# A feed-forward part with Strassen products: weight and token loads move from SyncE's DMA queue to GpSimd's, and forms and down pieces change their place in the order

## The chip, the cores and the metric

The kernel runs on one core of a Trainium2 chip. The metric is device time in microseconds of one execution, the median of three runs. One more execution was taken by the hardware profiler, and all rows below come from it.

## The reference

One inference step of a one-layer decoder trunk, all in float32: 2048 prompt tokens and 8 sample tokens (one for each of 8 sequences with 16384 cached positions in pages of 128).

```python
def layer(x, pos, conv_prev, chunk_len, attend, p):
    proj = rmsnorm(x, p['g_mix']) @ p['w_in']
    u, v, c_q, c_kv, k_rope = ...            # gelu, rmsnorm and rope of slices of proj
    out_a = rmsnorm(spatial_gate(u, v, ...), p['g_out_a'])
    out_b = rmsnorm(attend(q_nope, q_rope, c_kv, k_rope), p['g_out_b'])
    x = x + jnp.concatenate([out_a, out_b], axis=-1) @ p['w_out']
    f, conv_new = conv_ffn(x, conv_prev, p['g_ffn'], p['w_up'], p['w_conv'], p['b_conv'], p['w_down'])
    return x + f, c_kv, k_rope, v, conv_new

def conv_ffn(x, conv_prev, g_ffn, w_up, w_conv, b_conv, w_down):
    up = rmsnorm(x, g_ffn) @ w_up                      # 1024 -> 2*2816
    xp = jnp.concatenate([conv_prev, up], axis=1)
    c = b_conv
    for k in range(3):                                 # causal depthwise convolution
        c = c + xp[:, k:k + T] * w_conv[k]
    gate, val = c[..., :2816], c[..., 2816:]
    return (jax.nn.silu(gate) * val) @ w_down, xp[:, -2:]
```

For the sample tokens `attend` reads all 8 x 128 cached pages, through a page table.

## The kernel before

Tokens lie on the free axis, features on the partitions. Each float32 operand of a large product is split in a high part (`hi`, a rounded copy by ScalarE, L86) and a low part (`lo = x - hi`, by VectorE or GpSimd, L126), and each product is three matmuls: hi x hi, hi x lo, lo x hi. The stages follow one another: input projection, attention, output projection, feed-forward.

**The sample stream.** The attention of the sample tokens is spread through all stages by `fill`, which takes a step of it whenever matmuls of a planned length have been written. Its pages come through SyncE's DMA queue: each `pump` issues 16 page loads (`ct`, later `cn`) as soon as slots are free, and the first of them waits in the queue until TensorE has read the pages that lay there. The stream ends with the third of the four token blocks below.

**The feed-forward part** takes the tokens in four blocks (`BL`; 512 each, the last 520) and the 2816 gate and value columns in 22 steps of 128 (`NF`). A *unit* is one step of one block, 88 in all. The two weight slices of a unit (gate `graw`, value in two halves `vraw`) and the two halves of a block form a 2 x 2 system that is computed with seven products instead of eight (Strassen): each product has a *form* of the weights (`wu`) and one of the tokens (`B11`, `T2`, ...). The token forms are made once a block by `load_h2`, while the last unit of the block before runs. The weight forms are made in each unit anew by `split_w`: VectorE makes two sums (L1380 and L1381), GpSimd two differences (L1406, L1407), and for each of seven forms ScalarE makes the high part and GpSimd the low one.

**The order is written out by hand**, and each engine takes its instructions in that order. In `up`, behind product j of unit q, `rest(j)` writes in this order: deferred work of the gate chain that falls due at this product (`flush`), loads that are due (`later`, `dlater`), then weight forms until `AHEAD` products ahead of j are covered, then as many *pieces* as `PIECES` says, then steps of side work. The sums belong to the first form of the next unit and stand where that form is made.

The gate chain of a unit spreads over its products and over the next unit's (slot 7 is product 0 of the next unit): bias and taps of the convolution, `silu`, then the gate product and `gh` (L2014, L86) and `gl` (L2023). For the second half of a block these last three are in slots 10, 10 and 11.

```python
            at_slot(10, lambda: gmul(1), lambda: ghi(1))
            at_slot(11, lambda: glo(1))
```

Each pair of units (even and odd) is followed by eight pieces of the down projection (`dp`): a piece is six matmuls into 128 of the 1024 output rows, out of two PSUM buffers, and VectorE adds it to `y` (L1775). Pieces need `gh` and `gl` of both units. Their weights come by `load_d` in four loads a pair (`draw`, two buffers) and are split by `split_d` (`wdh`, `wdl`). `split_d` follows every second piece, one product later, and `load_d` follows it, again one product later. The last pair of a block has its pieces in `ending` (or `last_pieces`).

Queues: `sp` is SyncE's, `gq` GpSimd's, `aq` ScalarE's. A DMA is issued in its place in its engine's order, and waits there until its target is free. In the feed-forward part SyncE's queue has all raw weights, the token loads of `load_h2`, the pages, the block's inputs `y`, and the stores and reloads of finished blocks. In the last block `late` reloads the finished blocks, normalises them and stores them, through the same queue.

Of the raw weights, the second value half of unit q+1 has the shortest way: its load is written one product after the fifth form of unit q, and the sums that read it two products after the load.

Of the kernel before, what the change touches and what calls it, by code (L numbers as in the profile page):

```python
# [26 lines left out]
NF = FF // 128  # L27
# [9 lines left out]
T0, T1, T2, T3 = -8, -3, 3, 0  # L37
# [14 lines left out]
def build(tc, A):  # L52
# [15 lines left out]
    sp, aq, gq = Queue(nc.sync), Queue(nc.scalar), Queue(nc.gpsimd)  # L68
# [55 lines left out]
    def split_to(hi, lo, src, lo_eng=None):  # L124
        copy(hi, src)
        (lo_eng or dve).tensor_sub(lo, src, f(hi))  # L126
# [11 lines left out]
    def kslot(shape, name, dt=F32):  # L138
        return kv.tile(shape, dt, tag="k", bufs=6, name=name)

    def qslot(shape, name, dt=F32):
        return kv.tile(shape, dt, tag="q", bufs=2, name=name)
# [20 lines left out]
    with ExitStack() as B:  # L163
# [11 lines left out]
        xs = wp.tile([128, 8, NS], F32, name="xs")  # L175
# [307 lines left out]
        for k in range(8):  # L483
# [18 lines left out]
            t = h0  # L502
# [403 lines left out]
    with ExitStack() as Ax:  # L906
# [123 lines left out]
        for i in range(16):  # L1030
# [17 lines left out]
            for j in (0, 1) if i == 0 else (i,) if i > 1 else ():  # L1048
                p = pm.tile([128, 512], F32, tag="mm", name="pu")
                proj_a(p, *(HA[1] if j == 1 else (hh, hl)), 0)  # L1050
                act.activation(us[:, j % 2, :], p, AF.Gelu, scale=RC[j][:, 0:1])
            p = pm.tile([128, 512], F32, tag="mm", name="pv")
# [87 lines left out]
    with ExitStack() as At:  # L1140
# [19 lines left out]
        def load_v(h, r):  # L1160
            vt[h, r] = v = sb.tile([128, 4, 128], F32R, tag="v", bufs=6, name="v")
            gq.dma_start(out=v, in_=v_sp[r * 512:r * 512 + 512, h, :].rearrange("(j p) e -> p j e", p=128))
            yield
# [130 lines left out]
        for i in range(NT + DONE + int(DN)):  # L1294
# [30 lines left out]
            if i == 14:  # L1325
                p = psT.tile([128, 512], F32, tag="t", name="spt")
# [15 lines left out]
                next(ahead, 0)  # L1342

    FORMS = ("B11", "T2", "B21", "T3", "T1", "T4", "B22")
    PIECES = ((0, 0, 0, 0, 1, 1, 1), (1, 1, 1, 1, 1, 0, 0))
    BL = [(0, 256), (512, 256), (1024, 256), (1536, 260)]
    NB, AHEAD = len(BL), 5
    NU = NB * NF
    GATE, VAL, TMP, wts, later, dlater = {}, {}, {}, {}, [], []
    at = {"g": 0, "v": 0, "w": 0, "dl": 0, "ds": 0}  # L1350

    def load_g():
        q = at["g"]
        at["g"] += 1
        if q < NU:
            GATE[q] = qslot([128, 8, 128], "graw")
            (sp if q else gq).dma_start(out=GATE[q], in_=A["w_up"][q % NF, 0])

    def load_v():
        if not at["v"]:  # L1360
            at["v"] = 2
            t = qslot([128, 8, 128], "vraw")
            gq.dma_start(out=t, in_=A["w_up"][0, 1])
            VAL[0], VAL[1] = t[:, 0:4], t[:, 4:8]
            return
        q, a = divmod(at["v"], 2)
        at["v"] += 1
        if q < NU:
            VAL[2 * q + a] = t = sb.tile([128, 4, 128], F32, tag="vr", bufs=3, name="vraw")
            sp.dma_start(out=t, in_=A["w_up"][q % NF, 1, :, 4 * a:4 * a + 4, :])  # L1370

    def form(src):
        w = kslot([128, 2, 4, 128], "wu", F32R)
# [44 lines left out]
    def load_d():  # L1418
        i = at["dl"]
        at["dl"] += 1  # L1420
        if i < 4 * NU // 2:
            p, m = divmod(i, 4)
            fi = 2 * p % NF
            DR[i] = t = sb.tile([128, 2, 2, 128], F32, tag="dr", bufs=2, name="draw")
            sp.dma_start(out=t.rearrange("p j m n -> p j (m n)"),
                         in_=A["w_down"][fi * 128:(fi + 2) * 128, m * 256:m * 256 + 256].rearrange("(j p) n -> p j n", p=128))

    def split_d():
        i = at["ds"]
        at["ds"] += 1  # L1430
        if i < 4 * NU // 2:
            if i % (2 * NF) == 2 * NF - 2 or i == 4 * NU // 2 - 1:
                w = kslot([128, 2, 2, 2, 128], "wd", F32R)
                hi, lo = w[:, 0], w[:, 1]
            else:
                hi, lo = (sb.tile([128, 2, 2, 128], F32R, tag=t, name=t) for t in ("wdh", "wdl"))
            split_to(hi, lo, DR.pop(i), pool)
            wts["d", i] = hi, lo
            dlater.append(load_d)
# [10 lines left out]
    with ExitStack() as Po:  # L1450
# [88 lines left out]
        for j, ci in enumerate(seq):  # L1539
            for m in range(8):  # L1540
                if j > 0 or m > 3:
                    p = pm.tile([128, 512], F32, tag="mm", name="op")
# [30 lines left out]
    with ExitStack() as Fx:  # L1573
# [9 lines left out]
        def parts(b):  # L1583
            return ends(b) if b == NB - 1 else ((0, 512),)
# [3 lines left out]
        def load_h2(b):  # L1588
# [6 lines left out]
            def src(k0, nk, h):  # L1595
                return x2_sp[k0 * 128:(k0 + nk) * 128, c0 + h * hm:c0 + h * hm + hm].rearrange("(k p) t -> p k t", p=128)

            def new(n, dt):
                tag = slots.pop(0)
                return sb.tile([128, 4, 260], dt, tag=tag, bufs=1, name=n), tag  # L1600

            def raw(n, k=slice(0, 4)):
                if n not in raws:
                    raws[n] = new("r" + n, F32)
                return raws[n][0][:, k, 0:hm]
# [27 lines left out]
            def free(n):  # L1633
                slots.extend(old[n])
# [12 lines left out]
            if b == 0:  # L1647
# [3 lines left out]
                xs = temps()  # L1651
# [20 lines left out]
                    lo(n, eng)  # L1672
                return
            free("B11")
            sp.dma_start(out=raw("B11"), in_=src(0, 4, 0))
            R = load_r()
            yield
            free("T2")
            yield
            free("B21")  # L1680
            sp.dma_start(out=raw("B21"), in_=src(4, 4, 0))
            yield
            free("T3")
            sp.dma_start(out=raw("T3"), in_=src(0, 4, 1))
            yield
            free("T1")
            for k in range(4):
# [2 lines left out]
            free("T4")  # L1690
            xs = temps()
            for i in range(2):
                sp.dma_start(out=xs[i], in_=src(4 + 2 * i, 2, 1))
            for k in range(4):
                scale(raw("B21", k), raw("B21", k), 4 + k, 0)
            yield
# [69 lines left out]
        def pieces(b, fi, gts):  # L1766
            for m in range(8):
                w = wd(b, fi, m)
                if m == 0:
                    gts = [G[i] for i in gts]  # L1770
                for o, nn in parts(b):
                    p = pd.tile([128, 512], F32, tag="d", name="dp")
                    mm3(p[:, 0:nn], [(*w(j), gt[0][:, o:o + nn], gt[1][:, o:o + nn]) for j, gt in enumerate(gts)])
                    y = Y[b][m][:, o:o + nn]
                    dve.tensor_add(y, y, p[:, 0:nn])  # L1775
                    fill(6 * nn / 2.4)
                if m % 2:
                    dlater.append(split_d)
                yield
# [183 lines left out]
        def up(b, fi, it, side, slow, hs):  # L1963
# [22 lines left out]
            def rest(j):  # L1986
# [5 lines left out]
                while at["w"] <= 7 * q + j + AHEAD and at["w"] < 7 * NU:  # L1992
                    split_w()
                take(it, PIECES[odd][j])
                take(side, 1)
# [94 lines left out]
        for b in range(NB):  # L2090
            if b == NB - 1:
                state = st["pool"].tile([128, 2 * NF, 3, NS], F32, tag="pg", bufs=st["slots"], name="state")
                sp.dma_start(out=state[:, :, 0:2, :], in_=A["state"])
                slow = late()
            for fi in range(NF):
                hs = none
                if fi == NF - 1 and b < NB - 1:
                    if b == NB - 2:
                        drain()
                    hs = load_h2(b + 1)  # L2100
                up(b, fi, it, side, slow if fi else none, hs)
                if b == 0 and fi == 0:
                    split_d()
                    split_d()
                if fi == 0 and b > 0:
                    take(load_y(b), 99)
                last2 = b * NF + fi - 1, b * NF + fi
                if fi % 2:
                    it = pieces(b, fi - 1, last2) if fi < NF - 1 else none
            split_d()  # L2110
            if b < NB - 1:
                it = ending(b, last2)
                for _ in range(8):
                    take(it, 1)
                    take(hs, 1)
                take(it, 99)
                take(hs, 99)
                it = none
                continue
            split_d()  # L2120
            assert next(slow, 0) == 0
            it = last_pieces(last2)
            act.activation(sb.tile([128, 1], F32, tag="tw", bufs=1, name="tw"), epst, AF.Sqrt)  # L2123
            take(it, 4)
            sp.dma_start(out=A["o_pconv"], in_=halo)
            sp.dma_start(out=A["o_sconv"][:, :, 0, :], in_=state[:, :, 1, :])
            sp.dma_start(out=A["o_sconv"][:, :, 1, :], in_=state[:, :, 2, :])
            take(it, int(T6) + int(TA) - 4)
            r0 = root(0)
            for _ in range(4):  # L2130
                take(r0, 1)
                take(it, 1)
            take(r0, 9)
            take(it, 99)
            for m in DA0:
                scale(0, m, dve, sp)
            half = [scale_pool(0, m, sp) for m in range(8) if m not in DA0 + DA1]
            for t in half:
                next(t)
            r1 = root(1)  # L2140
            take(r1, 1)
            for t in half:
                next(t, 0)
            take(r1, 99)
            for m in DA1:
                scale(0, m, dve, sp)
            for m in range(8):
                scale(1, m, pool if m in DA2 else dve, aq if m % 2 else sp)
# [97 lines left out]
```

## Time and profile before

| | |
|---|---|
| median of three runs | 3551.61 us (3549.71 to 3560.44) |
| the profiled execution's own time | 3551.91 us |
| its span | 3550.1 us |
| TensorE matmul busy | 3040.0 us (86%) |
| VectorE busy | 2178.8 us (61%) |
| GpSimd busy | 1792.2 us (50%) |
| ScalarE busy | 1609.0 us (45%) |
| mean granted TensorE clock | 0.92 |

Shares are of the span. The feed-forward part begins at about 1331 us (first up-projection matmul) and its last product at 3509 us. Waits on the chip are read as "engine, tile, line <- who released it: us in total, times, longest". A DMA queue has its engine's name with a q.

### The profile page before, as it was taken

What the parts mean: (1) busy time and instruction counts of PE and PEld (TensorE: products, weight loads), DVE (VectorE), ACT (ScalarE), POOL (GpSimd) and SP (SyncE); (2) the same over time, 40 slices, a digit from 0 to 9 for tenths busy, and PEclk for the clock granted to TensorE, in tenths of its full rate; (3) what the DMA queues carried; (4) which work ended last, traced back from release to release, by engine and by line L of the source; (5) the groups of instructions that cost most, each with busy time, mean ns of one, the idle gap of its engine ahead of it and who ended that gap; (6) DMA issues with size and microseconds to landing.
All of it is one profiled execution on the core that took longest, in us unless ns stands there. A gap on an engine that the chain in (4) does not pass through costs nothing. (4 is left out here: it accounts for less than half of the span.)

```text
span 3550.1 us, 71345 instructions
## 1 busy us (share of the span) xinstructions
PE 3040.0 (86%) x24340; PEld 2625.1 (74%) x24340; DVE 2178.8 (61%) x4367; ACT 1609.0 (45%) x4029; POOL 1792.2 (50%) x1665
## 2 busy tenths in 40 slices
PE   8998999999999987788877787887788888778787
PEld 7897887888777986667766676775676765777776
DVE  6565225777875437455547464656555556788886
ACT  4334335777874224343333343543443443445444
POOL 3342224222324547565655565755565665766664
PEclk9999999999999998889988898997898988889988
DMA  5447667888378995566667566267666643433332
GB/s 174 131 158 246 188 173 204 225 223 221 101 199 227 243 247 166 168 189 188 190 185 240 160 207 185 72 190 209 176 182 187 188 150 102 132 125 104 125 116 50
DMA packets 410760, 616.64 MB, mean 174 GB/s; under 512 B 69855, under 2 KB 300926, under 8 KB 410398
## 3 DMA queue, kind: packets, MB, share of 16 engines
q1 hardware_dynamic: 372560, 518.56, 49.5%
q0 software_dynamic: 26480, 87.14, 9.1%
q10 hardware_dynamic: 11358, 6.36, 0.6%
q8 instruction: 196, 3.21, 0.4%
q14 instruction: 166, 1.36, 0.1%
HBM read 547.58 MB, written 64.28 MB: 172 GB/s over the span
## 5 line engine op out<-in xcount | busy, mean ns | idle before, releaser
L76 PE MATMUL dp<-gh,wdh 128*128 128x512 f32 (+1 forms) x800 | 306.4, 383 | 210.7 <-ACT gh L86 178.6
L126 POOL TENSOR_TENSOR wu<-t,wu 128x512 fp32r<-128x512 f32 x264 | 353.7, 1340 | 211.0 <-ACT wu L86 211.0
L1757 DVE SCALAR_TENSOR_TENSOR c<-up,gn,c 128x256 f32<-128x256 f32 (+2 forms) x704 | 335.9, 482 | 153.5 <-ACT halo L1749 122.8
L76 PE MATMUL dp<-gl,wdh 128*128 128x512 f32 (+1 forms) x800 | 304.1, 380 | 84.2 <-DVE gl L2023 84.2
L126 POOL TENSOR_TENSOR wdl<-draw,wdh 128x512 fp32r<-128x512 f32 x171 | 224.6, 1314 | 260.2 <-ACT wdh L86 209.3
L126 POOL TENSOR_TENSOR wu<-vraw,wu 128x512 fp32r<-128x512 f32 x176 | 229.5, 1304 | 241.1 <-ACT wu L86 139.1
L76 PEld LDWEIGHTS dp<-gh,wdh 128*128 128x128 f32 x800 | 161.7, 202 | 243.7 <-ACT gh L86 194.2
L1775 DVE TENSOR_TENSOR y<-y,dp 128x512 f32<-128x512 f32 (+1 forms) x400 | 227.8, 578 | 156.8 <-PE dp L76 155.5
L126 POOL TENSOR_TENSOR wu<-graw,wu 128x512 fp32r<-128x512 f32 x176 | 244.9, 1392 | 130.4 <-ACT wu L86 120.5
L76 PE MATMUL dp<-gh,wdl 128*128 128x512 f32 (+1 forms) x800 | 295.0, 369 | 0.0
L1747 ACT ACTIVATE up<-halo 128x2 f32<-128x2 f32 x352 | 60.5, 172 | 448.2 <-DVE up L2026 448.1
L76 PE MATMUL s<-k,q 96*128 96x512 f32 (+2 forms) x960 | 254.7, 376 | 6.6 <-DVE S L1203 2.7
L76 PEld LDWEIGHTS dp<-gl,wdh 128*128 128x128 f32 x800 | 161.9, 202 | 112.2 <-DVE gl L2023 102.2
L86 ACT ACTIVATE gh<-c 128x256 fp32r<-128x256 f32 (+1 forms) x176 | 73.5, 418 | 376.3 <-DVE c L2014 376.3
L126 DVE TENSOR_TENSOR pl<-t,ph 128x512 fp32r<-128x512 f32 (+1 forms) x320 | 193.9, 606 | 53.1 <-ACT ph L86 49.4
L86 ACT ACTIVATE ph<-t 128x512 fp32r<-128x512 f32 (+1 forms) x320 | 170.0, 531 | 108.1 <-PE t L1227 103.6
L1380 DVE TENSOR_TENSOR t<-vraw 128x512 f32<-128x512 f32 x88 | 72.0, 818 | 227.5 <-DMA vraw<-in_w_up 142.9
L1215 ACT ACTIVATE S<-S,nm 128x512 f32<-128x512 f32 (+2 forms) x320 | 208.0, 650 | 6.8 <-POOL nm L1207 6.8
L1748 ACT ACTIVATE c<-up,gn 128x256 f32<-128x256 f32 (+1 forms) x352 | 199.0, 565 | 11.7
L76 PEld LDWEIGHTS s<-k,q 96*128 96x128 f32 x960 | 170.1, 192 | 46.0 <-DVE S L1203 11.1
L76 PE MATMUL up<-T4h,wu 128*128 128x256 f32 (+1 forms) x704 | 182.5, 337 | 1.4 <-DVE u L2026 1.2
L76 PEld LDWEIGHTS dp<-gh,wdl 128*128 128x128 f32 x800 | 163.1, 204 | 21.4
(458 smaller groups left out, 9425.1 us busy)
## 6 DMA issues: line engine op xcount, KB each, us to landing
ct<-in_cT SPq DMA_DIRECT2D x1024, 144.0 KB
cn<-in_cN SPq DMA_DIRECT2D x1024, 128.0 KB
draw<-in_w_down SPq DMA_DIRECT2D x176, 256.0 KB
vraw<-in_w_up SPq DMA_DIRECT2D x174, 256.0 KB
graw<-in_w_up SPq DMA_DIRECT2D x87, 512.0 KB
q_sp<-qs SPq DMA_DIRECT2D x48, 256.0 KB
ft<-x_sp SPq DMA_DIRECT2D x48, 256.0 KB
xt<-in_xT SPq DMA_DIRECT2D x16, 512.0 KB
```

The source lines that it names most:

```text
L76: pe.matmul(out, lhsT=w, rhs=x, start=start, stop=stop)
L86: act.activation(out, in_, AF.Copy)
L126: (lo_eng or dve).tensor_sub(lo, src, f(hi))
L1215: act.activation(s, s, AF.Exp, scale=SCALE, bias=d["nm"][:, qb:qb + 1], accum_out=d["ls"][:, qb, r:r + 1])
L1380: dve.tensor_add(TMP[1], A21, A22)
L1747: act.activation(p[:, 0:2], halo[:, ix, :], AF.Copy)
L1748: act.activation(c[:, 0:m], p[:, 2:2 + m], AF.Identity, scale=g(W_CONV, 4 * NF + ix), bias=g(B_CONV, ix))
L1757: dve.scalar_tensor_tensor(out=c[:, 0:npr], in0=p[:, j:j + npr], scalar=g(W_CONV, j * 2 * NF + ix), in1=c[:, 0:npr], op0=ALU.mult, op1=ALU ...
L1775: dve.tensor_add(y, y, p[:, 0:nn])
```

## The change

Raw weights (`graw`, `vraw`, `draw`) and the token loads of `load_h2` are issued by GpSimd instead of SyncE. The forms are made three products ahead instead of five. The pieces of a pair begin after product 5 of the even unit instead of product 4, and end after product 5 of the odd one. At the end of a block, loads that are due are issued before and after the last `split_d`.

```diff
-    PIECES = ((0, 0, 0, 0, 1, 1, 1), (1, 1, 1, 1, 1, 0, 0))
+    PIECES = ((0, 0, 0, 0, 0, 1, 1), (1, 1, 1, 1, 1, 1, 0))
-    NB, AHEAD = len(BL), 5
+    NB, AHEAD = len(BL), 3
     # load_g
-            (sp if q else gq).dma_start(out=GATE[q], in_=A["w_up"][q % NF, 0])
+            gq.dma_start(out=GATE[q], in_=A["w_up"][q % NF, 0])
     # load_v
-            sp.dma_start(out=t, in_=A["w_up"][q % NF, 1, :, 4 * a:4 * a + 4, :])
+            gq.dma_start(out=t, in_=A["w_up"][q % NF, 1, :, 4 * a:4 * a + 4, :])
     # load_d
-            sp.dma_start(out=t.rearrange("p j m n -> p j (m n)"),
+            gq.dma_start(out=t.rearrange("p j m n -> p j (m n)"),
     # load_h2, likewise for B21, T3 and the two xs
-            sp.dma_start(out=raw("B11"), in_=src(0, 4, 0))
+            gq.dma_start(out=raw("B11"), in_=src(0, 4, 0))
     # after the last unit of a block
+            while dlater:
+                dlater.pop(0)()
             split_d()
+            while dlater:
+                dlater.pop(0)()
```

## Rows read from the trace of the kernel before

**Rows 1.** Windows: length; busy PE, PEld, DVE, ACT, POOL; clock; DMA share; GB/s.
```profile
1362.00:1885.00 523.00, 430.29 (x3780) 369.26 (x3780) 295.45 (x578) 209.22 (x573) 310.82 (x241) 0.90 0.64 189
1905.00:2420.00 515.00, 411.25 (x3669) 359.52 (x3668) 289.83 (x568) 216.80 (x583) 306.09 (x236) 0.90 0.57 172
2450.00:2960.00 510.00, 416.47 (x3052) 340.06 (x3052) 288.41 (x536) 205.25 (x561) 307.69 (x241) 0.89 0.59 175
3050.00:3500.00 450.00, 360.41 (x2609) 342.74 (x2608) 366.22 (x708) 217.68 (x597) 302.14 (x229) 0.89 0.33 108
```

**Rows 2.** Waits of TensorE (PE) from 1340 to 3512 us.
```profile
PE dp L76 <- ACT gh L86: 178.6, 42, 14.0
PE dp L76 <- DVE gl L2023: 84.2, 49, 3.8
PE up L76 <- DVE u L2026: 40.0, 15, 7.9
...
PE up L76 <- POOL wu L126: 0.3, 1, 0.3
```

**Rows 3.** Waits of TensorE in the last block, 3050 to 3500 us.
```profile
PE dp L76 <- DVE gl L2023: 40.5, 20, 2.8
PE dp L76 <- ACT gh L86: 26.0, 13, 2.6
```

**Rows 4.** Waits of VectorE (DVE) from 1340 to 3512 us.
```profile
DVE t L1380 <- DMA vraw<-in_w_up: 142.9, 24, 10.4
...
DVE t L1380 <- issue: 75.0, 15, 12.6
```

**Rows 5.** Timeline of SyncE's queue: start us, length us, DMA, count.
```profile
1764.56 6.61 SPq L66 DMA_DIRECT2D draw<-in_w_down  x3
1771.77 9.73 SPq L66 DMA_DIRECT2D ct<-in_cT  x16
...
1782.06 0.86 SPq L66 DMA_DIRECT2D vraw<-in_w_up  x2
```

**Rows 6.** Timeline of all engines after that; in brackets the idle time before.
```profile
1787.08 0.69 DVE L1380 TENSOR_TENSOR t<-vraw 128x512 f32<-128x512 f32 x1 [11.64 <-issue]
...
1789.74 0.79 PE L76 MATMUL dp<-gh,wdh 128*128 128x512 f32 x1 [13.00 <-ACT gh L86]
...
1793.12 0.42 PE L76 MATMUL up<-T4l,wu 128*128 128x256 f32 x1
...
1797.55 0.28 PE L76 MATMUL up<-B22l,wu 128*128 128x256 f32 x1
```

**Rows 7.** Waits of SyncE's queue (SPq) from 1340 to 3512 us.
```profile
SPq L66 <- POOL wdl L126: 277.5, 92, 19.2
```

**Rows 8.** DMA issues: queue, count, KB each, us to landing.
```profile
draw<-in_w_down SPq DMA_DIRECT2D x176, 256.0 KB
vraw<-in_w_up SPq DMA_DIRECT2D x174, 256.0 KB
graw<-in_w_up SPq DMA_DIRECT2D x87, 512.0 KB
...
k<-kn_sp POOLq DMA_DIRECT2D x32, 256.0 KB, 5.8
```

**Rows 9.** Timeline of TensorE: first matmuls of a product, a piece, a product.
```profile
1708.77 0.28 PE L76 MATMUL up<-T1h,wu 128*128 128x256 f32 x1
...
1710.19 0.39 PE L76 MATMUL dp<-gh,wdh 128*128 128x512 f32 x1
...
1711.60 0.28 PE L76 MATMUL up<-T4h,wu 128*128 128x256 f32 x1
```

**Rows 10.** Instructions by tile and line, GpSimd's issues: min/median/max ns.
```profile
L66 POOL DMA_DIRECT2D graw<-in_w_up x1: 558/558/558, 1303.6 to 1303.6; - x1
...
L66 POOL DMA_DIRECT2D v<-v_sp x32: 747/796/832, 565.4 to 1034.5; - x32
```

**Rows 11.** Costliest groups: a form's low part; busy us, mean ns, idle before.
```profile
L126 POOL TENSOR_TENSOR wu<-t,wu 128x512 fp32r<-128x512 f32 x264 | 353.7, 1340 | 211.0 <-ACT wu L86 211.0
```

More of the change, by code (lines that the diff above doesn't have):

```diff
@@ L1680, in load_h2 @@
             free("B21")
-            sp.dma_start(out=raw("B21"), in_=src(4, 4, 0))
+            gq.dma_start(out=raw("B21"), in_=src(4, 4, 0))
             yield
             free("T3")
-            sp.dma_start(out=raw("T3"), in_=src(0, 4, 1))
+            gq.dma_start(out=raw("T3"), in_=src(0, 4, 1))
             yield
@@ L1692, in load_h2 @@
             for i in range(2):
-                sp.dma_start(out=xs[i], in_=src(4 + 2 * i, 2, 1))
+                gq.dma_start(out=xs[i], in_=src(4 + 2 * i, 2, 1))
             for k in range(4):
```

## The prediction

> **What bounds the kernel now.** I read the page's busy table and slices first: TensorE is the fullest engine from end to end, so what counts is where it stands still and for whom. The feed-forward part runs from 1340 to 3512 us, 2172 us or 24.7 us for each of its 88 units. [rows 1] give the middle of its four blocks: in the first TensorE works 430 of 523 us, and no engine is fuller. The 93 us it is idle are the target; the next two blocks have 104 and 94, the last, without page loads, 90 (and there VectorE is busy 366 of 450 us). [rows 2] name the releasers over the whole part: 178.6 us before a down-projection matmul for ScalarE's `gh`, 84.2 us for VectorE's `gl`, 40.0 us before an up-projection matmul for VectorE's `u`, and 0.3 us for a form (`wu`). 66.5 us of the first two fall in the last block, in steps of at most 2.8 us [rows 3]; in the other three blocks they are longer, up to 14.
>
> Who makes `gh` late there is in [rows 4]: VectorE waits 142.9 us in 24 waits, and 75.0 us in 15 more that are put down to nothing, before L1380, the sum of two raw weight halves. What holds the load is one example in [rows 5] and [rows 6]. SyncE's queue first sits in three `draw` loads for 6.61 us (over the part it waits 277.5 us for GpSimd's `wdl` [rows 7]), then issues 16 page loads in 9.73 us, and only at 1782.06 comes to the `vraw` that VectorE has been waiting for since 1775.4. The sum starts at 1787.08, 5.0 us after that issue. Of a wait of 11.64 us, 6.6 passed before the load was even issued. Behind the sum in VectorE's order stand the gate product and `gl` of the unit before, so TensorE stands for 13.00 us and then runs at its lower clock: at 1793.12 a 256-column matmul takes 0.42 us, at 1797.55 again 0.28.
>
> **The queue.** The change takes 176 `draw`, 174 `vraw` and 87 `graw` issues [rows 8] and 15 token loads (three blocks of five) from SyncE. After it SyncE keeps pages, `y`, `x3` and output moves, so the 9.73 us of pages and the waits for page slots no longer stand ahead of a weight. On GpSimd every load stands behind GpSimd's own last reader of its slot, so it adds no long wait there; what `vraw` still waits for is landing. The nearest row is a 256 KB load issued by GpSimd among the pages of the attention part, 5.8 us [rows 8].
>
> **The order.** With five products of lead, the sum for unit q+1 is queued after product 2 of unit q, ahead of the previous unit's gate product (slot 10, after product 3) and `gl` (slot 11, after product 4). With three it is queued after product 4, behind both. So even a late `vraw` no longer delays `gh` and `gl`; behind it now stand the first `y` additions, and two PSUM buffers of the down product cover those. The pieces start after product 5 instead of 4. A product is 12 matmuls and takes 1.42 us, a piece of six takes 1.41 (1708.77 to 1710.19 to 1711.60) [rows 9]. So `gl` gets 1.42 us more, against waits of 84.2/49 = 1.7 us on average; a `gh` wait without page trouble is 26.0/13 = 2.0 us. Part of each can remain.
>
> **What it adds.** 261 weight loads of the `graw` kind at 0.558 us [rows 10], 176 `draw` with two runs per partition and 15 token loads with four, between 0.558 and the 0.796 of `v` [rows 10]; I take 0.63 and 0.77: 146 + 111 + 12 = 269 us, 3.05 us per unit of GpSimd's time. GpSimd now works 311/22 = 14.1 us per unit [rows 1], so it comes to 17.2 of some 23. On average this hides in the 212 us that it is idle in a block of 523. It does not hide everywhere. From product 6 of an odd unit to product 5 of the next no piece stands in between: seven products at 1.42 us (as many as before, one later), while GpSimd needs 17.2/7 = 2.45 us per product where it needed 2.0. Three forms instead of five are ready at the start; the fourth to seventh then come at 2.45, 4.9, 7.35 and 9.8 us, and are wanted at 4.3, 5.7, 7.1 and 8.5. With ScalarE's half of each form ahead of it and forms of 1.34 us [rows 11], that is 1.3 us late at best and about 3 with the two subtractions in the run; page matmuls standing among the products win back about half. I take 1.5 us per pair of units, 44 x 1.5 = 66 us. Bounds: 0, since GpSimd's idle time can cover it all, and 269 for all issue time on the path plus 44 x 2 x 1.42 = 125 for the two products of lost lead, 394. I stay near the low end because waits for forms are only 0.3 us today [rows 2].
>
> **The sum,** against the profiled execution's 3551.9 us (span 3550.1; the median of three runs is 3551.6, so nothing is to be shifted):
> - `gh` and `gl`: 178.6 + 84.2 = 262.8 us. I take 85%, -223. Bounds -263 and -130 (landing still late and VectorE in the last block, at 366 of 450 us, unable to follow).
> - Clock: the granted clock of the blocks is 0.89 to 0.90 [rows 1]. After the 13 us stand some 7 us ran at the lower level, 3.5 us lost. The last block, with waits of 2 us, has no better clock, so I count only seven such stands, -25. Bounds 0 and -75.
> - Forms late: +66 (0 to +394).
> - Block edges and PSUM buffers. The first two units of a block have no pieces, so GpSimd sets their pace with 2 x 3.05 us more, and token loads on GpSimd wait for TensorE's last reader of their slot. One waits for the last piece, which now comes in the same step, and queues forms behind it. +22, that is 5.5 us per block. Bounds: 0 as these products may wait for VectorE anyway, and +60, half as much again as the 40.0 us for `u`.
>
> -223 - 25 + 66 + 22 = -160, so **3392 us**, 4.5% faster. The case reaches from 3300 (the waits gone, half of the late forms) to 3500.
>
> A rule that speaks against this. The Trainium skill, "DMA: Bandwidth & Descriptors", section "Rules for kernel authors", says that spreading DMAs over SP, ACT and GpSimd does not help bandwidth, as they share 16 engines, and that only the sequencer's issue time is saved. By its first half rival 2 below is what happens; its second half is what [rows 5] show, 9.73 us of issue time ahead of a load that lands in 5.0. I hold with the second, since the share of the DMA engines in the blocks with pages is 0.57 to 0.64 [rows 1].
>
> **Rivals.**
> 1. *GpSimd becomes the pace, slower.* Each load on GpSimd stands between two forms, the lead is two products shorter, and the bare run of seven products outruns it in every pair. Place: products 3 to 5 of even units. Price: the whole 394 us against 223 + 25, 3551.9 + 146 = about 3698; it decides from 248/88 = 2.8 us per unit. For: 3.05 us per unit of issue is above that. Against: GpSimd's idle time, and pieces that stretch the other products to 2.8 us, above its 2.45. Chance 0.12.
> 2. *The transfers themselves are late.* If 16 shared engines and not the queue make `vraw` late, it arrives no earlier, and pages issued without a break crowd it more. Then only the reordering pays: `gl` waits and the last block's `gh`, 84.2 + 26.0 = 110, against 66 + 22 of costs: 3551.9 - 22 = 3530. For: DMA busy 0.64, and even units with only two bare products, 2.8 us, from issue to sum. Against: the 5.0 us of [rows 5, 6]. Chance 0.12, half of it within 0.3%.
> 3. *The gain is fuller.* No forms late, clock at its bound: 3551.9 - 263 - 75 + 22 = 3236. For: the reorder separates load and gate chain completely. Against: GpSimd's 17.2 us per unit. Chance 0.10.
>
> My own case has 0.66. A measurement of this kernel tells about 0.3% from no change. Faster: 0.66 + 0.10 + 0.06 = 0.82; same 0.06; slower 0.12. The range runs from just below my own case up to rival 2 and leaves out rival 1 and most of rival 3: 3290 to 3530.
>
> **What would show it.** In the profile after, SyncE has no weight loads and GpSimd has 452 more issues of 0.55 to 0.8 us; its busy time in a block rises by about 60 us. The waits of L1380 for `vraw` may keep some us, but TensorE's waits for `gh` and `gl` fall from 263 to about 40, also where `vraw` is late. New rows "`up` from `wu`" of about 66 us should stand at products 3 to 5 of even units. If `up` from `wu` is over 250 us, rival 1 holds; if L1380 still waits 200 us and `gh` too, rival 2. I am wrong if the time is above 3530, or if it falls while `gh` and `gl` keep their waits.

## The result, and the profile after

The changed kernel takes 3461.95 us (median of three runs, 3461.78 to 3470.41) against 3551.61, a ratio of 0.9749 with a 95% interval of 0.9715 to 0.9783. It is 90 us faster where 160 were predicted; 3392 was the forecast, 3290 to 3530 the range. The profiled execution after took 3470.41 us with a span of 3468.6.

First the waits of TensorE over the feed-forward part of the kernel after, which answer to [rows 2]:

```profile
PE up L76 <- POOL wu L126: 123.2, 115, 4.0
PE dp L76 <- DVE y L1775: 70.5, 42, 3.9
PE up L76 <- DVE c L1757: 34.2, 24, 6.0
PE up L76 <- ACT wu L86: 25.9, 34, 3.2
```

The two waits that were to go are gone: `gh` (178.6 before) has no row among the largest and `gl` (84.2) has 5.8 us. In their place stand forms that come late, 123.2 us for GpSimd's half and 25.9 for ScalarE's, and `y` and `c`. These two were already there before, smaller (same part, kernel before):

```profile
PE dp L76 <- DVE y L1775: 31.7, 26, 4.5
...
PE up L76 <- DVE c L1757: 14.7, 12, 3.7
```

VectorE's waits before the sum L1380, which answer to [rows 4], fell from 227.5 us (the two rows there and 9.6 us in two small ones) to 67 (these three rows and 6.4 us in two small ones):

```profile
DVE t L1380 <- DMA vraw<-in_w_up: 29.2, 15, 5.5
DVE t L1380 <- issue: 23.2, 14, 5.2
DVE t L1380 <- POOL wu L126: 8.1, 4, 3.7
```

The windows in the middle of the four blocks (length; busy PE, PEld, DVE, ACT, POOL; clock; DMA share; GB/s) answer to [rows 1]:

```profile
1372.00:1840.00 468.00, 419.17 (x3777) 364.48 (x3775) 328.09 (x556) 203.68 (x562) 362.98 (x343) 0.95 0.70 203
1880.00:2350.00 470.00, 419.40 (x3708) 366.82 (x3709) 328.17 (x573) 218.19 (x586) 368.04 (x346) 0.94 0.64 186
2395.00:2850.00 455.00, 403.24 (x2985) 329.79 (x2986) 323.60 (x519) 197.53 (x553) 351.74 (x334) 0.94 0.69 188
2935.00:3400.00 465.00, 364.95 (x2527) 346.44 (x2527) 405.08 (x686) 210.88 (x579) 344.15 (x318) 0.90 0.32 104
```

In the three blocks with page loads TensorE is idle for 49 to 52 us where it was 93 to 104, and the granted clock rose from 0.89 or 0.90 to 0.94 or 0.95. In the last block it is idle for 100 us of 465 where it was 90 of 450, and VectorE is busy for 405 of 465 us. Its waits answer to [rows 3]; not one of those two rows is left, and a larger one has come:

```profile
PE dp L76 <- DVE y L1775: 66.1, 39, 3.9
PE up L76 <- POOL wu L126: 24.2, 24, 3.4
```

The loads after, with the median time from issue to landing last, answer to [rows 8]; the second fence has GpSimd's issues in the first block (busy us, mean ns):

```profile
graw<-in_w_up POOLq DMA_DIRECT2D x88, 512.0 KB, 4.7
draw<-in_w_down POOLq DMA_DIRECT2D x176, 256.0 KB, 4.0
vraw<-in_w_up POOLq DMA_DIRECT2D x174, 256.0 KB, 4.5
```

```profile
L66 POOL DMA_DIRECT2D draw<-in_w_down x41 | 29.9, 729 | 0.0
L66 POOL DMA_DIRECT2D vraw<-in_w_up x42 | 23.2, 552 | 0.0
```

So the span fell by 81.5 us: TensorE's idle time by 95.6 (510.1 to 414.5), while its busy time rose by 14.1 (3040.0 to 3054.1).

### The profile page after: what moved, and what is told of

It is laid out like the page before. It is cut to its first block, busy times and chain, and to the rows that moved or that the text cites. A ratio compares the mean times of both kernels' runs of the same rounds, so it can differ in the third digit from the quotient of the medians.

```text
span 3468.6 us, 70928 instructions
## 1 busy us (share of the span) xinstructions
PE 3054.1 (88%) x24340; PEld 2640.2 (76%) x24340; DVE 2376.0 (68%) x4367; ACT 1607.2 (46%) x4029; POOL 2046.0 (59%) x2117
## 5 line engine op out<-in xcount | busy, mean ns | idle before, releaser
L126 POOL TENSOR_TENSOR wu<-t,wu 128x512 fp32r<-128x512 f32 x264 | 343.8, 1302 | 378.7 <-ACT up L1747 255.1
L1757 DVE SCALAR_TENSOR_TENSOR c<-up,gn,c 128x256 f32<-128x256 f32 (+2 forms) x704 | 337.5, 481 | 67.4 <-ACT halo L1749 47.7
L76 PE MATMUL dp<-gh,wdh 128*128 128x512 f32 (+1 forms) x800 | 292.0, 365 | 70.6 <-DVE y L1775 70.5
L76 PE MATMUL dp<-gl,wdh 128*128 128x512 f32 (+1 forms) x800 | 288.7, 361 | 5.8 <-DVE gl L2023 5.8
L76 PE MATMUL dp<-gh,wdl 128*128 128x512 f32 (+1 forms) x800 | 287.7, 360 | 0.7 <-POOL wdl L126 0.7
L76 PE MATMUL up<-T3h,wu 128*128 128x256 f32 (+1 forms) x704 | 173.5, 324 | 99.9 <-POOL wu L126 78.4
L126 POOL TENSOR_TENSOR wu<-graw,wu 128x512 fp32r<-128x512 f32 x176 | 234.5, 1333 | 6.9 <-ACT wu L86 5.2
L76 PEld LDWEIGHTS up<-T3h,wu 128*128 128x128 f32 x704 | 131.4, 216 | 118.1 <-POOL wu L126 87.8
L76 PE MATMUL up<-T2h,wu 128*128 128x256 f32 (+1 forms) x704 | 164.6, 312 | 46.4 <-DVE c L1757 34.0
L2014 DVE TENSOR_TENSOR c<-c,c 128x256 f32<-128x256 f32 (+1 forms) x176 | 189.1, 1074 | 1.9 <-ACT c L2010 1.9
L1380 DVE TENSOR_TENSOR t<-vraw 128x512 f32<-128x512 f32 x88 | 142.6, 1620 | 67.2 <-DMA vraw<-in_w_up 29.2
```

What stands on the lines that cost most here:

```text
L76: pe.matmul(out, lhsT=w, rhs=x, start=start, stop=stop)
L1380: dve.tensor_add(TMP[1], A21, A22)
L1757: dve.scalar_tensor_tensor(out=c[:, 0:npr], in0=p[:, j:j + npr], scalar=g(W_CONV, j * 2 * NF + ix), in1=c[:, 0:npr], op0=ALU.mult, op1=ALU ...
L2014: dve.tensor_mul(x, c[0, h][:, 0:hm], x)
```

## The experiments

The best view of all the runs is the length of each block. A block is counted here from the start of its first token form (`B11h`, L1625 on ScalarE) to that of the next block, the last one to the end of the span; "start" is the time of the first such form, and what lies ahead of it is the same code except for the first loads. All in us, from one profiled execution each, so that differences of a few us between single blocks are not to be read; the ratio is that of the timed runs to the kernel before on the same chip, with its interval.

| kernel | pieces | lead | weights issued by | start | 1 | 2 | 3 | last | ratio |
|---|---|---|---|---|---|---|---|---|---|
| before | old | 5 | SyncE | 1329.9 | 550.8 | 556.5 | 561.0 | 551.9 | 1 |
| after | new | 3 | GpSimd | 1341.1 | 505.9 | 513.0 | 521.6 | 587.0 | 0.9749 |
| e1_queue | old | 5 | GpSimd | 1338.6 | 545.1 | 545.1 | 558.3 | 575.5 | 1.0042 (1.0022 to 1.0062) |
| e2_order | new | 3 | SyncE | 1338.3 | 539.0 | 518.7 | 520.0 | 559.5 | 0.9732 (0.9712 to 0.9753) |
| e3_lead | old | 3 | SyncE | 1329.5 | 560.4 | 544.2 | 548.4 | 551.7 | 0.9986 (0.9976 to 0.9996) |
| e4_pieces | new | 5 | SyncE | 1331.0 | 520.7 | 521.1 | 531.5 | 534.8 | 0.9682 (0.9666 to 0.9698) |
| e5_queue_pieces | new | 5 | GpSimd | 1341.9 | 506.6 | 506.4 | 531.1 | 560.1 | 0.9689 (0.9661 to 0.9717) |
| e6_lead4 | new | 4 | SyncE | 1338.6 | 535.5 | 513.9 | 533.2 | 562.6 | 0.9778 (0.9747 to 0.9809) |
| e7_last_sync | new | 3 | GpSimd, last block SyncE | 1339.8 | 502.6 | 510.6 | 520.1 | 558.5 | 0.9658 (0.9631 to 0.9684) |
| e8_queue_pages | new | 5 | GpSimd, last block and first loads SyncE | 1331.5 | 509.2 | 508.2 | 520.6 | 534.0 | 0.9593 (0.9564 to 0.9621) |
| e9_vraw | new | 5 | as e8, of these only `vraw` | 1329.8 | 498.6 | 497.2 | 505.2 | 534.1 | 0.9490 (0.9459 to 0.9521) |
| e10_vraw_act | new | 5 | as e9, ScalarE for GpSimd | 1332.4 | 519.3 | 520.4 | 565.9 | 535.4 | 0.9793 (0.9755 to 0.9832) |
| e11_queue_no_taps | new | 5 | as e5, L1760 left out | 1336.1 | 507.4 | 508.0 | 525.5 | 550.4 | 0.9665 (0.9601 to 0.9728) |
| e12_no_taps | new | 5 | as e8, L1760 left out | 1334.0 | 508.8 | 509.5 | 527.6 | 507.7 | 0.9529 (0.9481 to 0.9576) |

All of them keep the change's two loops around the last `split_d` of a block; no run tried these alone. The start is not the same for the same code: e2 and e6, with SyncE, begin at 1338 us, after code that did not change. What the queue does to the start is one row: `R`, which VectorE needs for the first token forms, stands behind three `vraw` and two `draw` issues on GpSimd, and VectorE waits 12.69 us for it in the kernel after instead of 7.83 before.

**e1_queue: the queue alone.**

```diff
-    PIECES = ((0, 0, 0, 0, 0, 1, 1), (1, 1, 1, 1, 1, 1, 0))
-    NB, AHEAD = len(BL), 3
+    PIECES = ((0, 0, 0, 0, 1, 1, 1), (1, 1, 1, 1, 1, 0, 0))
+    NB, AHEAD = len(BL), 5
```

> Only the queue is changed: weights and token loads on GpSimd, forms five products ahead and pieces at their old place. Theory A (queue and order each take part of the stall: the queue makes the load earlier, the order takes the sums out from in front of the gate chain): VectorE's waits before L1380 fall from 226 us to about 60, TensorE's waits for gh to about 90 us, those for gl stay at about 84; the first three blocks take about 530 us each against 551 to 561 before and 506 to 522 after; the last stays at about 552, since its order is the old one; whole time 3490 us. Theory B (the queue alone does it): the time of the changed kernel or less, 3440 to 3465. Theory C (the order alone does it): 3545 or more. For the last block, which became 35 us longer: if GpSimd's DMA issues slow VectorE there, it takes 580 us or more here too; if it is the place of the sums beside GpSimd's forms, it stays under 560.

Measured: 3566.18 us, slower by 0.4%, as theory C had it. TensorE still waits 186.4 us for `gh`. The timeline shows what holds the load now (start, length, engine, line; in brackets the idle time before):

```profile
1648.00 1.50 POOL L126 TENSOR_TENSOR wu<-t,wu 128x512 fp32r<-128x512 f32 x1
1649.46 0.56 POOL L66 DMA_DIRECT2D vraw<-in_w_up  x1
1650.04 1.27 POOL L126 TENSOR_TENSOR wu<-graw,wu 128x512 fp32r<-128x512 f32 x1
1652.72 0.69 DVE L1380 TENSOR_TENSOR t<-vraw 128x512 f32<-128x512 f32 x1 [4.37 <-issue]
...
1655.38 0.80 PE L76 MATMUL dp<-gh,wdh 128*128 128x512 f32 x1 [5.44 <-ACT gh L86]
```

The issue of `vraw` comes when GpSimd has worked off the forms in front of it; VectorE stands for 4.37 us and TensorE for 5.44. Over the part L1380 waits 166 us instead of 227.5. The three page blocks are 20 us shorter, the last is 24 us longer (between the two expectations) and the start 9 us later.

**e2_order: both moves in the order, all loads on SyncE.**

```diff
-            gq.dma_start(out=t, in_=A["w_up"][q % NF, 1, :, 4 * a:4 * a + 4, :])
+            sp.dma_start(out=t, in_=A["w_up"][q % NF, 1, :, 4 * a:4 * a + 4, :])
...
```

> Only the order is changed: forms three products ahead, pieces one product later, all loads on SyncE as before. Theory A: L1380 still waits about 200 us for its load, but TensorE's waits for gh and gl go to under 30 us in all; part comes back as waits for y and for forms; the first three blocks take about 530 us, the last about 585 as in the changed kernel (VectorE's sums meet GpSimd's forms there): 3510 us. Theory B: 3545 or more. Theory C: 3440 to 3465, with blocks of 506 to 522 us.

Measured: 3457.97 us, as fast as the whole change and inside theory C. L1380 still waits 156 us, but `gh` and `gl` are not delayed by it any more (`gl` 3.9 us, `gh` none): the order alone takes them off the path. The waits that come instead are those of the kernel after:

```profile
PE up L76 <- POOL wu L126: 93.2, 104, 3.0
PE dp L76 <- DVE y L1775: 80.4, 46, 6.8
PE up L76 <- DVE c L1757: 65.8, 27, 10.5
```

**e3_lead: the lead of three alone,** loads on SyncE, old PIECES.

> Only the lead of the forms is cut from five products to three; pieces and queue as before. Theory A: the sums now stand behind gh and gl in VectorE's order, so a late load no longer delays them, and gh waits fall from 179 us to about 60; the gl waits stay at 84 or grow, since the pieces begin as early as before; new waits for forms about 50 us; last block 570 to 587 us if the place of the sums is what lengthens it: 3530 us. If a cut lead only costs (the rival), 3590 or more.

Measured: 3547.59 us, 0.14% under the kernel before, and between the two expectations. `gh` is nearly gone here too (2.4 us), `gl` keeps 54.3 of its 84.2 us, and nothing is gained: the waits have changed places.

```profile
PE up L76 <- POOL wu L126: 87.6, 78, 3.0
PE up L76 <- ACT up L1747: 68.7, 30, 6.8
PE dp L76 <- DVE y L1775: 55.7, 30, 7.4
```

**e4_pieces: the later pieces alone,** loads on SyncE, lead 5.

> Only the pieces are moved one product later; lead of five products and queue as before. Theory A: the gl waits (84 us) go and each gh wait is shorter by 1.4 us (42 of them, about 60 us), but the long waits behind a late load stay, about 120 us; L1380 waits as before, 220 us; last block about 530 us, shorter than before, since there all waits are short: 3460 to 3490 us. If the lead is what lengthens the last block, this one has no long last block; if the place of the pieces does it, it takes about 585 us here too and the time is 3530.

Measured: 3438.9 us, below the expectation. One product of delay for the pieces gives 3.2%, more than the whole change. `gh` falls only to 121.4 us and `gl` to 69.3, with L1380 waiting almost as long as before (214 us); TensorE's idle time falls from 510 to 423 us, and all four blocks get shorter, by 30, 35, 30 and 17 us.

**e5 to e8: the parts on top of the pieces.** e5 is the change with `AHEAD` 5; e6 has the pieces with `AHEAD` 4 and SyncE; e7 and e8 are these, e8 with `AHEAD` 5 and the token loads on SyncE as well:

```diff
-            gq.dma_start(out=GATE[q], in_=A["w_up"][q % NF, 0])
+            (gq if q < 3 * NF else sp).dma_start(out=GATE[q], in_=A["w_up"][q % NF, 0])
     # load_v, here as in e8 (in e7 without the 1 <)
-            gq.dma_start(out=t, in_=A["w_up"][q % NF, 1, :, 4 * a:4 * a + 4, :])
+            (gq if 1 < q < 3 * NF else sp).dma_start(out=t, in_=A["w_up"][q % NF, 1, :, 4 * a:4 * a + 4, :])
     # load_d, likewise
-            gq.dma_start(out=t.rearrange("p j m n -> p j (m n)"),
+            (gq if 1 < i < 6 * NF else sp).dma_start(out=t.rearrange("p j m n -> p j (m n)"),
```

> The change with its lead put back to five products: GpSimd's queue and the later pieces. Theory P (the later pieces carry the gain; the queue only moves the issue into GpSimd's order, which is worth some 20 us where pages flow and costs some 25 in the last block and 8 at the start, as in e1_queue): the pieces alone took 3438.9, e1_queue added 12, so 3440 to 3455, and VectorE's sum L1380 still waits over 120 us. Rival Q (with the pieces out of the way, the queue is the second half of the gain and the shorter lead is what spoilt it in the change): under 3425.

> Later pieces, lead of four products, weights and tokens on SyncE. Lead 5 gave 3438.9, lead 3 gave 3458.0. Theory C (a shorter lead puts VectorE's sum L1380 beside GpSimd's form, where it took 1776 ns in the median of the last block instead of 679, and leaves forms late): waits of up for wu between 10 and 50 us, 3440 to 3455. Rival (lead 5 still holds the gate chain behind late sums, gh and gl 191 us; lead 4 queues the sum behind the gate product, so these fall under 80 us without late forms): below 3425.

> The change with the weights of the last block alone issued by SyncE again; all else as in the change (3461.95; its last block 587 us in the profile, 560 with SyncE's queue in e2_order). Theory P: in the last block no pages stand in SyncE's queue, so GpSimd's 53 us of issue time bring nothing and cost the 27 us: last block 555 to 565, 3430 to 3440. Rival (the last block is long because of the shorter lead, whatever the queue): last block over 575, 3455 or more.

> Later pieces with a lead of five, weights issued by GpSimd only in the three blocks with pages; the loads ahead of the first product, the last block's weights and all token loads on SyncE. Theory P: the start and the last block as with the pieces alone (535 us), the three page blocks some 20 us shorter together as e1_queue was against before: 3415 to 3430. Rival (with the pieces moved, the wait for pages is off the path and GpSimd's issue time is pure cost): 3440 to 3465.

Measured: e5 3445.44, e6 3477.63, e7 3433.04, e8 3407.12 us. GpSimd's queue shortens the three page blocks by 35 us together (e8 against e4) and lengthens the last one by 26 (e5 against e8) or 28.5 (after against e7), at either lead; the gain in the page blocks is more than e8's theory P had. The shorter lead does next to nothing in the page blocks (e7 against e8) and costs 25 us in the last (558.5 against 534.0; e2 against e4 likewise). e5 and e7 came out where their theory P had put them.

e6 came out above both neighbours, against both expectations. It is the cleanest look at the order: with a lead of four the sum stands behind the gate product and ahead of `gl`, and of the two waits exactly `gl` is left, in waits of up to 11.8 us.

```profile
PE dp L76 <- DVE gl L2023: 160.8, 38, 11.8
PE dp L76 <- DVE y L1775: 61.2, 38, 4.8
```

What the lead does to the last block is to be read in L1380 there (busy us, mean ns). First before, then e2_order, then after:

```profile
L1380 DVE TENSOR_TENSOR t<-vraw 128x512 f32<-128x512 f32 x20 | 13.6, 680 | 0.0
```

```profile
L1380 DVE TENSOR_TENSOR t<-vraw 128x512 f32<-128x512 f32 x21 | 36.2, 1723 | 0.0
```

```profile
L1380 DVE TENSOR_TENSOR t<-vraw 128x512 f32<-128x512 f32 x20 | 50.0, 2501 | 4.9 <-POOL late L1832 2.4 <-POOL wu L126 1.2 <-DMA vraw<-in_w_up 0.8
```

The same operation on tiles of the same shape takes 0.68, 1.72 and 2.50 us in the mean. With a lead of three VectorE's sum falls beside GpSimd's forms nearly every time (median 1776 ns in e2_order); with a lead of five it does not, whichever engine loads (679 ns in e1_queue and e5). Longer sums by themselves do not lengthen the block: in e3, with the old pieces, the median is 1773 ns and VectorE is busy 37 us longer than before (468.4 against 431.3), and yet the last block takes 551.7 us against 551.9. The 25 us come only with the later pieces.

**e9_vraw and e10_vraw_act: which load needs another queue, and whose.**

```diff
     # load_d, and load_g likewise
-            (gq if 1 < i < 6 * NF else sp).dma_start(out=t.rearrange("p j m n -> p j (m n)"),
+            sp.dma_start(out=t.rearrange("p j m n -> p j (m n)"),
     # e10 besides, load_v
-            (gq if 1 < q < 3 * NF else sp).dma_start(out=t, in_=A["w_up"][q % NF, 1, :, 4 * a:4 * a + 4, :])
+            (aq if 1 < q < 3 * NF else sp).dma_start(out=t, in_=A["w_up"][q % NF, 1, :, 4 * a:4 * a + 4, :])
```

> As e8_queue_pages (3407.1), but of the three blocks with pages only vraw is issued by GpSimd; draw and graw are SyncE's again. Theory V (what counts is that vraw, the load behind which VectorE's sum and the gate chain stand, is not behind pages and draws; the other issues only cost GpSimd time, 0.73 us a draw): L1380 waits no more than the 106 us of e8_queue_pages, 3390 to 3410. Rival (draw and graw late behind pages cost as much): form or wdh waits appear, 3420 to 3440, as with the pieces alone (3438.9).

> As e9_vraw, but those vraw are issued by ScalarE. Theory G (on GpSimd the load still comes late because it stands in order behind GpSimd's forms, and takes GpSimd's time; ScalarE is busy 0.44 of a block and would issue it sooner): L1380's waits fall under 60 us, 3375 to 3400. Rival (the issue waits for the slot's last reader, a form of GpSimd, on whatever engine; on ScalarE the evacuations of up stand behind that wait): new waits of up for ScalarE over 40 us, 3415 or more.

Measured: e9 3369.03 us, faster than both kernels and below its expectation; e10 3475.51. The waits before L1380 in e8 and then in e9:

```profile
DVE t L1380 <- DMA vraw<-in_w_up: 65.0, 16, 9.8
DVE t L1380 <- POOL wu L126: 27.3, 6, 5.2
DVE t L1380 <- issue: 13.7, 4, 5.6
```

```profile
DVE t L1380 <- DMA vraw<-in_w_up: 35.3, 14, 8.5
DVE t L1380 <- issue: 0.2, 1, 0.2
```

With `draw` and `graw` back on SyncE, `vraw` comes earlier on GpSimd: each page block is 11 to 15 us shorter. These two loads had no need of another queue; on GpSimd they only stood in front of `vraw` and of the forms. In e10 L1380 waits even less, 24 us, so the load is earlier still, as theory G had it; but the time is worse than with the pieces alone, all of the difference in the third block (565.9 us against 531.5), and not for the rival's reason (`up` waits only 9.5 us for ScalarE's `s` in the page blocks). New is a wait for pages:

```profile
PE po L76 <- DMA cn<-in_cN: 54.9, 27, 4.6
```

SyncE's page loads take longer to issue while ScalarE issues too: 16 of them take about 10 us in e9 and about 14 in e10, in the median of 66 such groups each. Start and length of some in e9, then in e10:

```profile
2352.00 9.48 SPq L66 DMA_DIRECT2D cn<-in_cN  x16
2373.48 10.00 SPq L66 DMA_DIRECT2D cn<-in_cN  x16
```

```profile
2429.45 14.22 SPq L66 DMA_DIRECT2D cn<-in_cN  x16
...
2477.49 21.86 SPq L66 DMA_DIRECT2D cn<-in_cN  x16
```

SyncE's waits in e10 are put down to the landing of a `vraw` in 96 cases, 366.9 us in all. Why a load of another queue should hold SyncE up was not tried. The waits for pages are about half of the 106 us between e9 and e10; in 42 more TensorE is busy, and why stays open too.

**e11_queue_no_taps and e12_no_taps: why the queue costs in the last block.** In e5's last block VectorE is busy 22.4 us longer than in e8's, and one line makes it up, L1760 (e5, then e8):

```profile
L1760 DVE SCALAR_TENSOR_TENSOR c<-state,gn,c 128x8 f32<-128x8 f32 x86 | 92.9, 1080 | 1.5
```

```profile
L1760 DVE SCALAR_TENSOR_TENSOR c<-state,gn,c 128x8 f32<-128x8 f32 x86 | 70.2, 816 | 1.5
```

A timeline of e5 shows such a stretch:

```profile
3001.22 0.73 POOL L66 DMA_DIRECT2D draw<-in_w_down  x1
...
3001.97 1.31 POOL L126 TENSOR_TENSOR wu<-vraw,wu 128x512 fp32r<-128x512 f32 x1
3002.42 3.64 DVE L1760 SCALAR_TENSOR_TENSOR c<-state,gn,c 128x8 f32<-128x8 f32 x2
3003.22 1.29 POOL L126 TENSOR_TENSOR wdl<-draw,wdh 128x512 fp32r<-128x512 f32 x1
3004.46 1.30 POOL L126 TENSOR_TENSOR wu<-t,wu 128x512 fp32r<-128x512 f32 x1
3005.70 0.56 POOL L66 DMA_DIRECT2D graw<-in_w_up  x1
```

After an issue GpSimd has three operations ready and runs them without a gap, and two operations of eight columns on VectorE take 3.64 us; they end when GpSimd comes to its next issue. The next two kernels leave L1760 out:

```diff
-            if m > npr:
+            if m < npr:
                 for j in range(2):
```

> As e5_queue_pieces, but L1760, the two taps of the kept state over the last block's eight sample columns (86 calls on VectorE, 128x8), is left out, so those columns lack it. In e5_queue_pieces it took 92.9 us in all, up to 4.6 us for a pair, against 70.2 in e8_queue_pages, whose last block is 26 us shorter. Theory K (GpSimd's issues make it run its forms back to back, and a VectorE operation that meets them stands until they end; that is the 26 us): last block within 8 us of that of e12_no_taps. Rival T (GpSimd's 57 us more work make forms and pieces late by themselves): last block 20 to 30 us longer than that of e12_no_taps.

> As e8_queue_pages, with L1760 left out in the same way. Last block 534 in e8_queue_pages. If VectorE's time sets the last block, it gets 20 to 60 us shorter; if it does not, under 10. The comparison with e11_queue_no_taps: theory K within 8 us, rival T 20 to 30 us.

Measured: last block 550.4 us in e11 and 507.7 in e12, which is 26 us shorter than e8's 534.0, after taking 46 us of work from VectorE: with the later pieces VectorE's time does count in this block. But the two differ by 43 us, more than either theory said. The slow place has moved, to `gl` and L1380 (e11, then e12):

```profile
L2023 DVE TENSOR_TENSOR gl<-c,gh 128x260 fp32r<-128x260 f32 (+1 forms) x45 | 61.8, 1373 | 1.0 <-ACT gh L86 1.0
L1380 DVE TENSOR_TENSOR t<-vraw 128x512 f32<-128x512 f32 x21 | 23.0, 1095 | 12.8 <-DMA vraw<-in_w_up 12.3 <-issue 0.3
```

```profile
L2023 DVE TENSOR_TENSOR gl<-c,gh 128x260 fp32r<-128x260 f32 (+1 forms) x45 | 38.7, 860 | 0.5 <-ACT gh L86 0.5
L1380 DVE TENSOR_TENSOR t<-vraw 128x512 f32<-128x512 f32 x21 | 15.7, 746 | 10.0 <-DMA vraw<-in_w_up 9.3 <-issue 0.8
```

These two are 30 us longer in sum with the queue on GpSimd. That the queue costs 24 to 43 us in the last block is shown by four pairs of kernels (e1 against before, e5 against e8, after against e7, e11 against e12). That meetings of VectorE and GpSimd are its cause fits these rows, and one more: VectorE's L1757, which has one of its inputs in PSUM, takes 481 or 482 ns in all of before, after, e1 to e5, e8 and e9, while the lines that got longer (L1380, L1760, L2023) have both in SBUF. But taking one line away did not take the cost away, so how much of it is the added work on GpSimd by itself stays open.

## Where the prediction was right and where it was wrong

The direction was right and the time lies inside the range, but in good part by luck: the prediction gave the gain to the load that comes earlier and to the gate chain that is freed, and the later pieces were an aside. Measured, the later pieces alone give more than the whole change (0.9682 against 0.9749), the queue together with the shorter lead takes a little back, and the time is inside because the range reaches to 3530.

From the ratios the change comes apart in a chain of kernels (in us of 3553):

| step | from, to | us |
|---|---|---|
| pieces one product later | before, e4 | -113 |
| `vraw` of the page blocks on GpSimd | e4, e9 | -68 |
| `draw` and `graw` of the page blocks on GpSimd | e9, e8 | +37 |
| the last block, the first loads and the tokens on GpSimd | e8, e5 | +34 |
| lead of three for five | e5, after | +21 |
| sum | | -89 |

The sizes belong to this order of steps: the lead alone, with the old pieces, was worth nothing (e3). The first step has the two loops in it; e1 and e3 have them too and gain next to nothing, so the pieces are the likely cause of the 113 us. The last step is the least certain (the intervals of e5 and after touch) and is shown better by the last blocks.

- **What bounds it:** right. TensorE's waits set the time, and `gh` and `gl` left the path.
- **The queue:** the step that failed is "On GpSimd every load stands behind GpSimd's own last reader of its slot, so it adds no long wait there; what `vraw` still waits for is landing". It lands in 4.5 us, but it is issued late, behind GpSimd's forms and behind 0.73 us for each `draw`. As the change has it, the queue gives the page blocks 20 to 37 us (e1 against before, e5 against e4, after against e2) and takes about as much in the last block and at the start. The reading of [rows 5] was right for one of three loads: `vraw` alone on GpSimd is worth 68 us.
- **The order:** right that the sum behind the gate chain frees `gh` and `gl`: e2 shows it with `vraw` as late as ever, e6 between the two. Wrong that this is a gain by itself; in e3 the wait went to `wu`, `up` and `y`. Wrong too that two PSUM buffers cover the `y` additions behind the sum: TensorE's waits for `y` rose from 31.7 to 70.5 us, 66.1 of them in the last block, and those for `c` from 14.7 to 34.2; the sum has no term for these 58 us. The lead brings the waits for `y`: 55.7 to 80.4 us in the kernels with a lead of three or four, 7.2 to 38.0 in those with five, whichever engine loads. The pieces, for which I counted 1.42 us more for `gl` and no more, carry the gain: -113 us by themselves. That the whole gate chain gets one product more in every pair is how I read it.
- **`gh` and `gl`, -223:** measured -257 (262.8 to 5.8). But the time is not in these two waits: e9 keeps 155 us of them (81.9 and 73.0) and is 93 us faster than the change.
- **Forms late, +66:** mis-sized; 123.2 + 25.9 = 149 us. The place was right: 112 of the 149 us stand at products 3 to 5 of even units, 108 of them before T3 and T4. I had put 1.5 us on a pair of units; it came to 149/44 = 3.4.
- **Clock, -25:** the granted clock did rise in the page blocks, but TensorE's busy time in these blocks fell by only 7 us (1341.8 to 1334.4) and rose by 16 in the last one (427.6 to 443.6), 14 us up over the span. So the gain is not to be found there; why stays open (in e9 it is 42 us below before).
- **Block edges, +22:** the start came 11 us later. 4.9 of them are the wait for `R`; the other 6 come from code that did not change, as in e2. What the edges of the other blocks cost was not read apart.
- **The last block:** I expected it to get shorter. It is 35 us longer: 25 for the lead (e2 against e4) and 27 for the queue (after against e2), less 17 for the pieces (e4 against before). I had VectorE's 366 of 450 us as a bound only, not as a term.
- **Rivals:** 1 is out (149 us of late forms, not 394). 2 is out in its mechanism, since 256 KB land in 4.0 to 4.5 us and L1380 waits 67 us, not 200, yet it named the right pattern: queue and order together gave no more than the order, e2. 3 is out, since forms do come late.

One operation of VectorE, L1380, took 0.68 us, then 1.72 and 2.50 when it met GpSimd's forms, and two eight-column operations took 3.64 us beside three of GpSimd's. The Trainium skill has the rule in "SBUF — State Buffer", section "Who interferes with whom": a VectorE instruction with two inputs in SBUF contends with a GpSimd instruction that reads SBUF, for a port pair that is an exclusive lock. The traces agree, in the durations just given.

One load that no longer stands behind page issues was worth 68 us (e9), and three loads on GpSimd's queue together with its order brought nothing over the order alone (e2). The Trainium skill says in "DMA: Bandwidth & Descriptors", section "Rules for kernel authors", that spreading loads over issuing engines saves only issue time. e9 agrees, as L1380's waits fell from 214 us (e4) to 35.5; in e10 the issue time of `vraw` was saved as well, but SyncE's own issues took longer. The rule's other half, that spreading does not help bandwidth, no run here tests.

## What to carry to other kernels

When a load is late in a shared queue, move that load alone: its companions on the new engine stand in front of it and take that engine's time. An issue on a compute engine comes in the order of its compute, so look for what is in front of it there. Where two engines slow each other down, a changed lead can make every one of their operations meet; read the duration of the same operation before and after, not only the waits.

## What the hardware did that was not expected

- With weight issues on GpSimd VectorE's work takes longer. With the new pieces and a lead of five VectorE is busy 2179.2 us with no weight issue moved (e4), 2245.6 with 128 moved (e9), 2308.4 in e8 and 2325.7 with all of them (e5), for the same 4367 instructions.
- A lead of three instead of five does the same with no weight issue moved: 2266.2 us in e2 against 2179.2 in e4.
- ScalarE issues a `vraw` in 0.33 us against GpSimd's 0.55, and yet the kernel with 128 of them is 3.2% slower than with GpSimd's (3475.5 against 3369.0), and SyncE's page loads, 16 at a time, take about 14 us to issue instead of 10.
